# Sixteen meta tokens as full-height products over zeroed rows, in retention and in latent attention

## The chip, the cores and the metric

The kernel runs on one core of a Trainium2 chip. A core has a matrix engine (TensorE, written PE in the profile, with its weight loads listed apart as PEld), a vector engine (DVE), a scalar engine (ACT), a general engine (POOL) and a queue for transfers (SP). Each engine works through its own list of instructions in order and waits for others by semaphores. The metric is the time of one execution of the program on the device, in microseconds (us); lower is better.

## The reference

Two blocks run one after the other on 256 tokens of width 1024. The first has two layers, each with a feed-forward network, a mixer (gated delta rule in one layer, sliding-window attention in the other) and a second feed-forward network. The second block puts 16 learned "meta" tokens ahead of the 256 and has one layer: a mixer made of bidirectional retention (8 heads) and latent attention (8 heads) side by side, and a feed-forward network. Only the 256 real tokens are returned. The change touches the mixer of the second block alone:

```python
def _retention_dir(q, k, v, log_gamma, inclusive):      # o_i = sum_j gamma^(i-j) (q_i . k_j) v_j
    ...
    scores = jnp.einsum('bnihd,bnjhd->bnhij', qc, kc) * dmask
    inner = jnp.einsum('bnhij,bnjhe->bnihe', scores, vc)
    ...
def _mla_attention(q_nope, q_rope, k_nope, k_rope, v):
    ...
        s = jnp.einsum('bqhd,bkhd->bhqk', qn, k_nope) + jnp.einsum('bqhr,bkr->bhqk', qr, k_rope)
        p = jax.nn.softmax(s.astype(jnp.float32) * scale, axis=-1).astype(v.dtype)
        return jnp.einsum('bhqk,bkhd->bqhd', p, v)
def _mixer(...):
    ...
    y_ret = _head_group_norm(_bidir_retention(rq, rk, rv, decay_f, decay_b), gn_w)
    y_ret = (jax.nn.silu(rg) * y_ret) @ w_ret_out
    ...
    y_mla = _mla_attention(...).reshape(B, L, MLA_HEADS * MLA_DV) @ w_mla_out
    merged = jax.nn.sigmoid(a_gret) * y_ret + jax.nn.sigmoid(a_gmla) * y_mla
    return merged @ w_o
```

So every query looks at 272 keys: 256 real ones and 16 meta ones. In both mixers the last step of a head is a sum over those 272 keys, weights times values.

## The kernel before, in words

All activations live in on-chip memory, transposed (model dimension on the 128 partitions). Weights are streamed from memory in pieces of 512 columns. Each piece is split by ACT (`whi`, line 355) and DVE (`wlo`, line 356) into a high and a low part, and each linear layer (`lin`, lines 373 to 375) makes three products per 128 rows of weights: high by high, low by high, high by low. These triples are most of what TensorE does.

The mixer of the second block, `retention_mla`, has two parts. **Retention** goes over four pairs of heads. For a pair, `rope` turns keys and queries, `val` transposes the values of each head into a tile `rv` with three slices (128 keys, 128 keys, 16 meta keys), and `ret` makes the decayed scores, again with three slices, in a tile `ptr` of DVE's writing. The 16 meta rows of the second head of a pair sit 32 partitions further down than those of the first. `weigh` (line 1130) then sums over the keys: for each of two heads and two blocks of 128 queries, three products into one accumulating bank, over 128, 128 and 16 rows. An fp32 product is issued as two matmul records, so one `weigh` is 12 products and 24 records, and there are four of them. Group norm (`bn_stats` on DVE, a power on POOL) and `close` follow.

**Latent attention** goes over eight heads in an order written out by hand, `MLA_PLAN`: `s` scores and softmax of a head, `t` its transposition (the weights become `pt`, two slices of 128 keys copied by ACT at line 1339 and 16 meta rows copied by DVE at line 1340), `w` the weighing of one head (line 1350), and `y` one block of the retention output's linear layer. The plan names heads, so `w0` to `w7`. The weighing of a head is three products over 128, 128 and 16 rows, 64 columns of output and 256 queries, six records; the even head of a pair writes partitions 0 to 63 of a bank, the odd head 64 to 127. After the odd head, `split` makes `oh` and `ol` out of the bank. The scheduler of the language may move an instruction past others of its engine where it expects a wait.

The sliding-window attention of the first block has a weighing of the same kind (line 979): two heads into the two halves of a bank, each by products over 128 rows with 64 columns of output, there with 512 columns moved.

POOL has little to do. In this part it adds up squares for the norms (line 407), takes powers (line 383) and zeroes tiles (`MEMSET`).

Of the kernel before, what the change touches and what calls it, by code (L numbers as in the profile page):

```python
# [10 lines left out]
F32R = mybir.dt.float32r  # L11
I32 = mybir.dt.int32
AF = mybir.ActivationFunctionType
ALU = mybir.AluOpType
# [3 lines left out]
P = 128  # L18
D = 1024
KD = 8  # L20
S = 256
# [29 lines left out]
    "y0 s1 s0 y1 s6 t0 s2 t1 w0 w1 t2 s3 y2 s4 y3 t3 w2 w3 t4 s5 y4 w4 s7 t5 y5 t6 y6 t7 w5 w6 y7 w7"  # L51
# [170 lines left out]
def kernel(ctx: ExitStack, tc: tile.TileContext, dram: dict, out: bass.AP, dump=None):  # L222
# [79 lines left out]
    def tab(name, rows=P):  # L302
        o, w = _TABS[name]
        return tabs[:rows, o : o + w]
# [724 lines left out]
    def retention_mla(norm, stats, finish, dec, after):  # L1029
        xs = norm.xs  # L1030
        Y = [None] * H
        with home("mx") as gp:
            with home("ret") as rp:
# [20 lines left out]
                A.copy(rotr, tab("rot"))  # L1054
                metak = [[sb(rp, [P, 48], f"metak{j}{i}", F32R) for i in range(2)] for j in range(2)]
# [26 lines left out]
                def val(t, hh):  # L1082
# [6 lines left out]
                    o = sb(rp, [P, 3, P], f"rv{hh}", bufs=2)  # L1089
                    A.copy(o[:, 0:2, :], b[:, 0:2, :])  # L1090
                    A.copy(o[m - NM : m, 2, :], b[m - NM : m, 2, :])
                    return o
# [6 lines left out]
                def ret(p, k, q):  # L1099
# [3 lines left out]
                    for hh in range(2):  # L1103
# [7 lines left out]
                        pt = sb(rp, [P, 3, S], f"ptr{hh}", bufs=2)  # L1111
                        d3 = dec.t[2 * p + hh]
                        V.scalar_tensor_tensor(pt[:, 0:2, :], b, 64 ** -0.5, d3[:, 0:2, :], op0=ALU.mult, op1=ALU.mult)
                        pts.append(pt)
# [4 lines left out]
                    for hh in range(2):  # L1119
                        m = slice(32 * hh, 32 * hh + NM)  # L1120
                        V.scalar_tensor_tensor(pts[hh][m, 2, :], b[m, :], 64 ** -0.5, dec.t[2 * p + hh][m, 2, :], op0=ALU.mult, op1=ALU.mult)
# [34 lines left out]
                for p in range(4):  # L1156
# [13 lines left out]
                    vals[p] = val(v0, 0), val(v1, 1)  # L1170
# [29 lines left out]
            with home("mla") as rp:  # L1200
# [109 lines left out]
                PT, OB = {}, {}  # L1310
# [19 lines left out]
                def turn(h):  # L1330
# [7 lines left out]
                    pt = sb(rp, [P, 3, S], "pt", bufs=3)  # L1338
                    A.copy(pt[:, 0:2, :], b)
                    V.tensor_copy(pt[:NM, 2, :], bm)  # L1340
                    PT[h] = pt

                def weigh(h):
                    pr, hf = h // 2, h % 2
                    if hf == 0:
                        OB[pr] = bank(pm, [P, S])
                    o = OB[pr][hf * 64 : hf * 64 + 64, :]
                    for c in range(3):
                        m = P if c < 2 else NM
                        mm(o, VN[:m, c, h * 64 : h * 64 + 64], PT[h][:m, c, :], start=c == 0, stop=c == 2)  # L1350
                    if hf:
                        oh = sb(rp, [P, S], f"oh{pr}", F32R)
                        ol = sb(rp, [P, S], f"ol{pr}", F32R)
                        split(OB[pr], oh, ol)
                        MO.append((oh, ol))
# [184 lines left out]
```

## Time and profile before

| | |
|---|---|
| time before, median of 3 runs | 1481.27 us (1472.56 to 1790.16) |
| the profiled execution, its own time | 1473.83 us |
| its span, first to last instruction | 1472.0 us |
| granted TensorE clock, mean over the span | 0.995 |
| PE busy / DVE busy / ACT busy / POOL busy | 1443.5 / 1107.7 / 858.2 / 114.1 us |
| retention | about 1031 to 1127 us of the span |
| latent attention up to the end of the plan | about 1127 to 1204 us |
| gates, output and the last feed-forward network | about 1204 to 1472 us |

A busy time counts an instruction from its start to its end, and products overlap: a product of 0.28 us starts 0.11 us after the one before it. So a busy TensorE says little by itself. What a product costs is read from the distance of its start to the start of the next one, and below this distance is called its pitch.

### The profile page before, as it was taken

How to read it: one execution, taken by the hardware profiler on the slowest of the kernel's cores; microseconds unless marked ns; L12 is line 12 of the kernel's file. 1: busy time of each engine (PE TensorE's matmuls, PEld its weight loads, DVE VectorE, ACT ScalarE, POOL GpSimd, SP SyncE). 2: the span in 40 equal slices, each digit the busy share in tenths (PEclk: the TensorE clock that was granted, in tenths of full speed). 3: DMA queues.
4: the chain of work that ended last, by engine and by line, in shares of the span. 5: the costliest groups of instructions: out<-in, count | busy, mean ns of one | idle time of the engine just before them, and what ended most of it. 6: DMA issues, size and time to landing. Idle time of an engine off the chain costs nothing.

```text
span 1472.0 us, 31018 instructions
## 1 busy us (share of the span) xinstructions
PE 1443.5 (98%) x12318; PEld 1405.1 (95%) x12318; DVE 1107.7 (75%) x2340; ACT 858.2 (58%) x1767; POOL 114.1 (8%) x123
## 2 busy tenths in 40 slices
PE   8999999998999999999999999999999999999997
PEld 8999999988999999999997999999999889999997
DVE  6877668886877767777678877788877758777764
ACT  6655567655655555555547655665545756665552
POOL 2000141101100010000100100012001000100000
PEclk9999999999999999999999999999999999999998
DMA  7655443551555555555550555555432425555551
GB/s 254 224 195 201 171 148 116 166 167 33 181 191 198 201 189 185 201 195 187 193 199 30 201 178 195 177 196 172 134 113 91 144 87 195 207 199 187 193 197 58
DMA packets 46368, 248.34 MB, mean 169 GB/s; under 512 B 11408, under 2 KB 16272, under 8 KB 17168
## 3 DMA queue, kind: packets, MB, share of 16 engines
q1 hardware_dynamic: 45680, 245.87, 49.0%
q8 instruction: 97, 1.59, 0.4%
q10 hardware_dynamic: 544, 0.50, 0.1%
q14 instruction: 47, 0.39, 0.1%
HBM read 243.99 MB, written 2.36 MB: 167 GB/s over the span
## 4 chain that ended last, share of the span: by engine, by line
PE 86%; DVE 7%; ACT 2%; DMA 2%; issue 1%; POOL 1%; DVEq 0%; POOLq 0%; ACTq 0%; SPq 0%
PE bank L375 26%; PE bank L373 26%; PE bank L374 26%; DVE wlo L356 2%; PE bank L1130 1%; PE bank L1350 1%; DVE cv L652 1%; ACT whi L355 1%; PE bank L979 1%; DMA tc<-s 1%; PE bank L1319 1%; DVE xl L395 0%; DMA s<-tb 0%; PE bank L969 0%; POOL rr L383 0%
## 5 line engine op out<-in xcount | busy, mean ns | idle before, releaser
L356 DVE TENSOR_TENSOR wlo<-raw,whi 128x512 fp32r<-128x512 f32 x922 | 641.2, 700 | 257.4 <-ACT whi L355 255.9
L355 ACT CAST whi<-raw 128x512 fp32r<-128x512 f32 x922 | 565.4, 618 | 444.8 <-PE bank L375 407.3
L373 PE MATMUL bank<-xh,whi 128*128 128x256 f32 (+1 forms) x2488 | 697.0, 280 | 1.3 <-DVE xt L513 1.0
L374 PE MATMUL bank<-xh,wlo 128*128 128x256 f32 (+1 forms) x2488 | 692.9, 279 | 2.1 <-DVE wlo L356 2.1
L375 PE MATMUL bank<-xl,whi 128*128 128x256 f32 (+1 forms) x2488 | 692.3, 278 | 1.1 <-DVE xl L395 1.0
L374 PEld LDWEIGHTS bank<-xh,wlo 128*128 128x128 f32 x2488 | 468.5, 188 | 3.6 <-DVE wlo L356 3.1
L373 PEld LDWEIGHTS bank<-xh,whi 128*128 128x128 f32 x2488 | 466.9, 188 | 4.2 <-issue 2.1
L375 PEld LDWEIGHTS bank<-xl,whi 128*128 128x128 f32 x2488 | 466.9, 188 | 2.2 <-DVE xl L395 1.7
L375 PE MATMUL bank<-al,whi 128*128 128x256 f32 x880 | 243.8, 277 | 0.0
L373 PE MATMUL bank<-ah,whi 128*128 128x256 f32 x880 | 243.8, 277 | 0.0
L374 PE MATMUL bank<-ah,wlo 128*128 128x256 f32 x880 | 243.8, 277 | 0.0
L374 PEld LDWEIGHTS bank<-ah,wlo 128*128 128x128 f32 x880 | 165.9, 189 | 0.0
L375 PEld LDWEIGHTS bank<-al,whi 128*128 128x128 f32 x880 | 165.2, 188 | 0.0
L373 PEld LDWEIGHTS bank<-ah,whi 128*128 128x128 f32 x880 | 165.2, 188 | 0.0
L407 POOL TENSOR_TENSOR ssq<-sq,ssq 128x256 f32<-128x256 f32 (+1 forms) x72 | 63.8, 886 | 1080.4 <-ACT sq L406 1070.8
L378 ACT CAST ah<-ffu 128x256 fp32r<-128x256 f32 x110 | 44.7, 407 | 26.2 <-DVE ffu L482 26.1
L482 DVE TENSOR_TENSOR ffu<-ffg,ffu 128x256 f32<-128x256 f32 x110 | 46.7, 425 | 4.6 <-ACT ffg L481 1.2
L478 DVE TENSOR_TENSOR ffg<-bank,r 128x256 f32<-128x256 f32 x110 | 46.6, 424 | 2.8 <-PE bank L375 2.2
L481 ACT ACTIVATE ffg<-ffg 128x256 f32<-128x256 f32 x110 | 45.3, 414 | 5.7 <-DVE ffg L478 5.4
L480 DVE TENSOR_TENSOR ffu<-bank,r 128x256 f32<-128x256 f32 x110 | 46.6, 423 | 0.3
L379 DVE TENSOR_TENSOR al<-ffu,ah 128x256 fp32r<-128x256 f32 x110 | 46.0, 418 | 0.5 <-ACT ah L378 0.5
L373 PE MATMUL bank<-dec,whi 128*128 128x256 f32 x128 | 36.7, 286 | 0.0
(360 smaller groups left out, 1426.4 us busy)
## 6 DMA issues: line engine op xcount, KB each, us to landing
raw<-gu SPq DMA_DIRECT2D x109, 1024.0 KB, 4.8
raw<-dn SPq DMA_DIRECT2D x55, 1024.0 KB, 4.9
raw<-wret SPq DMA_DIRECT2D x12, 1024.0 KB, 4.9
raw<-aqk SPq DMA_DIRECT2D x8, 1024.0 KB, 4.8
raw<-wga SPq DMA_DIRECT2D x8, 1024.0 KB, 4.8
raw<-bin SPq DMA_DIRECT2D x6, 1024.0 KB, 4.9
raw<-az SPq DMA_DIRECT2D x4, 1024.0 KB, 4.8
raw<-av SPq DMA_DIRECT2D x4, 1024.0 KB, 4.9
```

The source lines that it names most:

```text
L355: A.copy(hi[:, :n], raw[:, o : o + n])
L356: V.tensor_tensor(lo[:, :n], raw[:, o : o + n], f32(hi[:, :n]), op=ALU.subtract)
L373: mm(o, wh, xh[:, :n], start=k == 0, stop=False)
L374: mm(o, wl, xh[:, :n], start=False, stop=False)
L375: mm(o, wh, xl[:, :n], start=False, stop=k == last)
L378: A.copy(hi, src)
L379: V.tensor_tensor(lo, src, f32(hi), op=ALU.subtract)
L407: G.tensor_tensor(acc[:, :n], q[:, :n], acc[:, :n], op=ALU.add)
L478: V.tensor_tensor(g, pg, r[:, :S], op=ALU.mult)
L480: V.tensor_tensor(u, pu, r[:, :S], op=ALU.mult)
L481: A.activation(g, g, AF.Silu)
L482: V.tensor_tensor(u, g, u, op=ALU.mult)
```

## The change

Both weighings get 128 rows in place of 16. The 16 meta rows move out of the third slices of `ptr`, `rv` and `pt` into tiles of their own, `metap` (weights) and `metav` (values), whose other rows are zeroed once by POOL: eight tiles for retention (two sets of two heads) and four for latent attention, where the third slice of the values `VN` is zeroed as well. In latent attention `w` now names a pair, and goes over the key slices outside and the two heads inside.

```diff
-    "y0 s1 s0 y1 s6 t0 s2 t1 w0 w1 t2 s3 y2 s4 y3 t3 w2 w3 t4 s5 y4 w4 s7 t5 y5 t6 y6 t7 w5 w6 y7 w7"
+    "y0 s1 s0 y1 s6 t0 s2 t1 w0 t2 s3 y2 s4 y3 t3 w1 t4 s5 y4 s7 t5 y5 w2 t6 y6 t7 y7 w3"
...
+                metap = [[sb(rp, [P, S], f"metap{j}{hh}") for hh in range(2)] for j in range(2)]
+                metav = [[sb(rp, [P, P], f"metav{j}{hh}") for hh in range(2)] for j in range(2)]
+                for t in metap[0] + metav[0] + metap[1] + metav[1]:
+                    G.memset(t, 0.0)
...
-                    A.copy(o[:, 0:2, :], b[:, 0:2, :])
-                    A.copy(o[m - NM : m, 2, :], b[m - NM : m, 2, :])
+                    A.copy(o, b[:, 0:2, :])
+                    mv = metav[p % 2][hh]
+                    A.copy(mv[m - NM : m, :], b[m - NM : m, 2, :])
...
-                            for c in range(3):
-                                m = slice(0, P) if c < 2 else slice(32 * hh, 32 * hh + NM)
-                                mm(bs[hh][:, i, :], pts[hh][m, c, i * P : i * P + P], rv[hh][m, c, :], start=c == 0, stop=c == 2)
+                            q = slice(i * P, i * P + P)
+                            for c in range(2):
+                                mm(bs[hh][:, i, :], pts[hh][0][:, c, q], rv[hh][0][:, c, :], start=c == 0, stop=False)
+                            mm(bs[hh][:, i, :], pts[hh][1][:, q], rv[hh][1], start=False, stop=True)
...
                 VN = sb(rp, [P, 3, 512], "vnat")
+                G.memset(VN[:, 2, :], 0.0)
+                metap = [sb(rp, [P, S], f"metap{j}") for j in range(4)]
+                for t in metap:
+                    G.memset(t, 0.0)
...
-                    A.copy(pt[:, 0:2, :], b)
-                    V.tensor_copy(pt[:NM, 2, :], bm)
-                    PT[h] = pt
+                    A.copy(pt, b)
+                    V.tensor_copy(metap[h % 4][:NM, :], bm)
+                    PT[h] = pt[:, 0, :], pt[:, 1, :], metap[h % 4]
...
-                def weigh(h):
+                def weigh(pr):
...
                     for c in range(3):
-                        m = P if c < 2 else NM
-                        mm(o, VN[:m, c, h * 64 : h * 64 + 64], PT[h][:m, c, :], start=c == 0, stop=c == 2)
-                    if hf:
...
+                        for hf in range(2):
+                            h = 2 * pr + hf
+                            mm(b[hf * 64 : hf * 64 + 64, :], VN[:, c, h * 64 : h * 64 + 64], PT[h][c], start=c == 0, stop=c == 2)
```

What this makes of the lists of the engines, at three places. On TensorE, at the weighing of the first pair of heads in retention, before (the products of `lin` around it are of the next pair's projections):

```order
L375 MATMUL bank_14498<-xl_2692_14140,whi_14517 128x272
L1130 MATMUL bank_14535<-rv_2752_14428,ptr_2762_14481 128x128 x6
L1130 MATMUL bank_14536<-rv_2754_14435,ptr_2764_14490 128x128 x6
L373 MATMUL bank_14567<-xh_2564_13369,whi_14568 128x256
```

The same place after:

```order
L375 MATMUL bank_14514<-xl_2692_14140,whi_14533 128x272
L1136 MATMUL bank_14551<-rv_2760_14444,ptr_2770_14497 128x128 x2
L1137 MATMUL bank_14551<-metav_2721_14294,metap_2717_14290 128x128
L1136 MATMUL bank_14551<-rv_2760_14444,ptr_2770_14497 128x128 x2
L1137 MATMUL bank_14551<-metav_2721_14294,metap_2717_14290 128x128
L1136 MATMUL bank_14552<-rv_2762_14451,ptr_2772_14506 128x128 x2
L1137 MATMUL bank_14552<-metav_2722_14295,metap_2718_14291 128x128
L1136 MATMUL bank_14552<-rv_2762_14451,ptr_2772_14506 128x128 x2
L1137 MATMUL bank_14552<-metav_2722_14295,metap_2718_14291 128x128
L373 MATMUL bank_14583<-xh_2564_13369,whi_14584 128x256
```

Nothing moves; the third product of each group reads other tiles. The other engines' lists in retention keep their order too, but for POOL's (below).

On TensorE, at the weighing of the first pair of heads in latent attention (`tabs,pe` are transpositions of the softmax weights, `dec,whi` products of the retention output's linear layer), after:

```order
L1349 MATMUL bank_16278<-tabs_81,pe_16172 128x128 x4
L1349 MATMUL bank_16279<-tabs_81,pe_16172 16x128 x2
L1361 MATMUL bank_16289<-pt_16260,vnat_15926 64x256
L375 MATMUL bank_16326<-dec_2877_15019,whi_16329 128x256
L1361 MATMUL bank_16289<-pt_16286,vnat_15926 64x256
L1361 MATMUL bank_16289<-pt_16260,vnat_15926 64x256
L1361 MATMUL bank_16289<-pt_16286,vnat_15926 64x256
L1361 MATMUL bank_16289<-metap_3074_15928,vnat_15926 64x256
L1361 MATMUL bank_16289<-metap_3075_15929,vnat_15926 64x256
L373 MATMUL bank_16326<-dec_2945_15350,whi_16345 128x256
```

Before, the six products stood together, three of one head and then three of the other, and the product of `lin` came behind them. Now one product of `lin` stands behind the first of the six, and the five behind it alternate between the heads. In the second pair three transpositions stand at that place; in the third and fourth pair the six stand together, behind a block of the linear layer.

On POOL, at the end of the feed-forward network ahead of retention, after (`ssq` are the sums of squares of the norm, `rms` its power):

```order
L407 TENSOR_TENSOR ssq_13378<-sq_14041,ssq_13378 128x272
L1059 MEMSET metap_2717_14290 128x256
L1059 MEMSET metap_2718_14291 128x256
L1059 MEMSET metav_2721_14294 128x128
L1059 MEMSET metav_2722_14295 128x128
L1059 MEMSET metap_2719_14292 128x256
L1059 MEMSET metap_2720_14293 128x256
L1059 MEMSET metav_2723_14296 128x128
L1059 MEMSET metav_2724_14297 128x128
L407 TENSOR_TENSOR ssq_13375<-sq_14145,ssq_13375 128x256
L407 TENSOR_TENSOR ssq_13378<-sq_14149,ssq_13378 128x272
L383 TENSOR_TENSOR rms_14154<-rms_14154,mhalf_85 128x8
```

The eight new `MEMSET` stand ahead of the last two sums of squares; before, nothing stood between the rows above and below them. The five new ones of latent attention (128x512 and four of 128x256) stand behind the `MEMSET` of 128x384 and ahead of two of 128x512 that were there before.

## Rows read from the trace of the kernel before

**Rows 1.** The page: busy time, share of the span and instructions of each engine.

```profile
PE 1443.5 (98%) x12318; PEld 1405.1 (95%) x12318; DVE 1107.7 (75%) x2340; ACT 858.2 (58%) x1767; POOL 114.1 (8%) x123
```

**Rows 2.** Stretches: length, then busy (count) of PE, PEld, DVE, ACT, POOL; clock; transfers.

```profile
580.00:730.00 150.00, 150.00 (x1326) 150.00 (x1325) 109.69 (x200) 86.52 (x160) 3.51 (x4) 1.00 0.57 194
850.00:1000.00 150.00, 150.00 (x1276) 150.00 (x1275) 117.42 (x224) 90.53 (x174) 8.50 (x8) 1.00 0.55 187
1035.00:1130.00 95.00, 95.00 (x753) 89.11 (x752) 75.79 (x198) 43.87 (x99) 5.57 (x8) 1.00 0.33 109
1204.00:1284.00 80.00, 80.00 (x707) 80.00 (x708) 64.91 (x123) 51.09 (x100) 5.19 (x7) 1.00 0.55 189
1284.00:1460.00 176.00, 176.00 (x1555) 176.00 (x1554) 123.59 (x227) 95.79 (x175) 6.34 (x7) 1.00 0.51 172
```

**Rows 3.** Timeline of PE, retention: first start, length to last end, line, form, count.

```profile
1042.34 4.18 PE L1130 MATMUL bank<-rv,ptr 128*128 128x128 f32 x24
1046.45 0.38 PE L373 MATMUL bank<-xh,whi 128*128 128x256 f32 x1
...
1042.56 0.39 PE L1130 MATMUL bank<-rv,ptr 128*128 128x128 f32 x2
1042.67 0.58 PE L1130 MATMUL bank<-rv,ptr 128*128 128x128 f32 x2
1042.88 0.37 PE L1130 MATMUL bank<-rv,ptr 16*128 16x128 f32 x1
1043.93 0.48 PE L1130 MATMUL bank<-rv,ptr 16*128 16x128 f32 x2
```

**Rows 4.** Timeline of PE, latent attention, the first pair and a single head.

```profile
1167.52 3.23 PE L1350 MATMUL bank<-pt,vnat 128*64 128x256 f32 x12
1170.67 0.39 PE L375 MATMUL bank<-dec,whi 128*128 128x256 f32 x1
...
1167.78 0.38 PE L1350 MATMUL bank<-pt,vnat 128*64 128x256 f32 x1
1168.00 0.38 PE L1350 MATMUL bank<-pt,vnat 128*64 128x256 f32 x1
1168.21 0.38 PE L1350 MATMUL bank<-pt,vnat 128*64 128x256 f32 x1
1168.52 0.42 PE L1350 MATMUL bank<-pt,vnat 16*64 16x256 f32 x1
...
1185.99 1.65 PE L1350 MATMUL bank<-pt,vnat 128*64 128x256 f32 x6
1187.57 0.95 PE L1319 MATMUL bank<-kf,qf 128*128 128x272 f32 x3
```

**Rows 5.** Timeline of PE, sliding-window attention, its weighing of one and of two heads.

```profile
803.45 1.07 PE L979 MATMUL bank<-pt,vn 128*64 128x512 f32 x2
804.45 0.33 PE L969 MATMUL bank<-tabs,pe 128*128 128x128 f32 x1
...
810.24 2.62 PE L979 MATMUL bank<-pt,vn 128*64 128x512 f32 x8
812.79 0.39 PE L373 MATMUL bank<-oh,whi 128*128 128x256 f32 x1
```

**Rows 6.** Timeline of ACT and DVE: the weights of the pair's second head are copied.

```profile
1167.40 0.59 ACT L1339 COPY pt<-bank 128x512 f32<-128x512 f32 x1 [0.69 <-PE bank L1337]
1167.91 0.40 DVE L1340 COPY pt<-bank 16x256 f32<-16x256 f32 x1
```

**Rows 7.** Timeline of PE and POOL: the end of the feed-forward network, and zeroing.

```profile
1015.10 0.28 PE L375 MATMUL bank<-al,whi 128*128 128x256 f32 x1
1017.03 1.54 POOL L407 TENSOR_TENSOR ssq<-sq,ssq 128x256 f32<-128x256 f32 x1 [3.16 <-ACT sq L406]
1021.13 0.74 PE L413 MATMUL bank<-ones,ssq 128*128 128x1 f32 x6 [0.70 <-POOL ssq L407]
1125.06 1.01 POOL L1278 MEMSET pt<- 128x512 f32 x2
```

More of the change, by code (lines that the diff above doesn't have):

```diff
@@ L1080, in rope, with val @@
                     return oh, ol
-                def val(t, hh):
+                def val(p, t, hh):
                     b = bank(pm, [P, 3, P])
@@ L1088, in val @@
                     nc.tensor.transpose(b[:m, 2, :], t[:, ST - m : ST], ident)
-                    o = sb(rp, [P, 3, P], f"rv{hh}", bufs=2)
-                    A.copy(o[:, 0:2, :], b[:, 0:2, :])
-                    A.copy(o[m - NM : m, 2, :], b[m - NM : m, 2, :])
-                    return o
+                    o = sb(rp, [P, 2, P], f"rv{hh}", bufs=2)
+                    A.copy(o, b[:, 0:2, :])
+                    mv = metav[p % 2][hh]
+                    A.copy(mv[m - NM : m, :], b[m - NM : m, 2, :])
+                    return o, mv
                 def gate(i, hh):
@@ L1110, in ret @@
                             mm(b[:, c, :], kl[rows, cs], qh[rows, :], start=False, stop=True)
-                        pt = sb(rp, [P, 3, S], f"ptr{hh}", bufs=2)
+                        pt = sb(rp, [P, 2, S], f"ptr{hh}", bufs=2)
                         d3 = dec.t[2 * p + hh]
-                        V.scalar_tensor_tensor(pt[:, 0:2, :], b, 64 ** -0.5, d3[:, 0:2, :], op0=ALU.mult, op1=ALU.mult)
-                        pts.append(pt)
+                        V.scalar_tensor_tensor(pt, b, 64 ** -0.5, d3[:, 0:2, :], op0=ALU.mult, op1=ALU.mult)
+                        pts.append((pt, metap[p % 2][hh]))
                     b = bank(pm, [48, S])
@@ L1120, in ret @@
                         m = slice(32 * hh, 32 * hh + NM)
-                        V.scalar_tensor_tensor(pts[hh][m, 2, :], b[m, :], 64 ** -0.5, dec.t[2 * p + hh][m, 2, :], op0=ALU.mult, op1=ALU.mult)
+                        V.scalar_tensor_tensor(pts[hh][1][m, :], b[m, :], 64 ** -0.5, dec.t[2 * p + hh][m, 2, :], op0=ALU.mult, op1=ALU.mult)
                     return pts
@@ L1169, in retention_mla @@
                     g0 = gate(6 * p + 4, 0)
-                    vals[p] = val(v0, 0), val(v1, 1)
+                    vals[p] = val(p, v0, 0), val(p, v1, 1)
                     g1 = gate(6 * p + 5, 1)
@@ L1309, in retention_mla @@
                 MO = []
-                PT, OB = {}, {}
+                PT = {}
                 def scores(h):
@@ L1337, in turn @@
                             nc.tensor.transpose(o, pe[:, i, c * P : c * P + m], ident)
-                    pt = sb(rp, [P, 3, S], "pt", bufs=3)
-                    A.copy(pt[:, 0:2, :], b)
-                    V.tensor_copy(pt[:NM, 2, :], bm)
-                    PT[h] = pt
-                def weigh(h):
[L1344 to L1347, printed above, removed]
-                    for c in range(3):
-                        m = P if c < 2 else NM
-                        mm(o, VN[:m, c, h * 64 : h * 64 + 64], PT[h][:m, c, :], start=c == 0, stop=c == 2)
-                    if hf:
[L1352 to L1355, printed above, removed]
+                    pt = sb(rp, [P, 2, S], "pt", bufs=3)
+                    A.copy(pt, b)
+                    V.tensor_copy(metap[h % 4][:NM, :], bm)
+                    PT[h] = pt[:, 0, :], pt[:, 1, :], metap[h % 4]
+                def weigh(pr):
+                    b = bank(pm, [P, S])
+                    for c in range(3):
+                        for hf in range(2):
+                            h = 2 * pr + hf
+                            mm(b[hf * 64 : hf * 64 + 64, :], VN[:, c, h * 64 : h * 64 + 64], PT[h][c], start=c == 0, stop=c == 2)
+                    oh = sb(rp, [P, S], f"oh{pr}", F32R)
+                    ol = sb(rp, [P, S], f"ol{pr}", F32R)
+                    split(b, oh, ol)
+                    MO.append((oh, ol))
                 YR = []
```

## The prediction

> **What bounds the kernel now.** I read the page first: TensorE has work for 98% of the span, the next engine, DVE, for 75% [rows 1]. A busy share does not say that TensorE is the bound, so the second view is the busy time by stretch, over the part that the change touches and what follows it [rows 2]. There TensorE has something in flight in every microsecond, at full clock, DVE is at four fifths and transfers at a third to a half. The reader is to see that work taken off TensorE's list here shortens the kernel, as long as its operands come in time. The third view is the timeline of TensorE at the two weighings, since what a product costs is its pitch, the distance to the next start.
>
> In retention, products over 128 rows start 0.11 us apart (1042.56, 1042.67), but the first one over 16 rows comes 0.21 after the last over 128, and from there to the first 16-row record of the next group are 1.05 us [rows 3]. A group is six records; at 0.11 each it would take 0.67. So 0.38 of each group goes to the changes from 128 to 16 rows and back. That it is the form and not a late operand is seen in the count: all four groups of a weighing have it, though only the first can wait for data. A whole weighing takes 4.11 us from its first start to that of the next product (1042.34 to 1046.45).
>
> In latent attention a record over 128 rows, 64 columns out and 256 columns moved has a pitch of 0.215 us (1167.78, 1168.00, 1168.21), and the step to the 16-row record is 0.31. A head of six records takes 1.58 us (1185.99 to 1187.57) and a pair 3.15 (1167.52 to 1170.67) [rows 4]: the two heads stand strictly behind each other. There are eight heads in five stretches, so 12.6 us in all.
>
> **The change part by part.**
>
> *Retention.* 32 of the 96 records get 128 rows. With nothing left to change form, a weighing is 24 records at 0.111, 2.66 us, in place of 4.11: 1.45 less. The first product of `lin` behind it is 0.38 long [rows 3], where another is 0.28 [rows 7]; I put that to the last change of form: 0.1. That is 1.55 us for each of four weighings, 6.2 us. Below nothing this term cannot go unless full rows cost more than 0.11, and the rows with full rows show 0.11; its bounds are 5.8 and 6.3.
>
> *Latent attention, rows.* Without the step to 16 rows and back a head would be six records at 0.215 and one exit: about 1.4 us.
>
> *Latent attention, two heads at once.* The two heads of a pair write different halves of the output partitions, so they use different columns of the array. Whether two such products run side by side is not seen at line 1350, where a 16-row record always stands between the heads. It is seen at line 979: one head's two records take 1.00 us (803.45 to 804.45), and two heads' eight records take 2.55 (810.24 to 812.79) [rows 5]. In line, eight records at twice the 0.215 of 256 columns, with an exit, would be 3.5 or more. So they do overlap there, and the second head's records must have run between the first head's. I take that for line 1350, whose shape differs only in moving 256 columns. A pair whose six products stand together is then one head's chain, 0.27 + 4 x 0.215 = 1.13, plus a start of the second head 0.1 to 0.25 later, plus an exit like the step above, 0.31: 1.6 us. That holds for the third and fourth pair, which stand behind a block of the linear layer.
>
> The first two pairs follow the transposition of their second head at once. Its weights are copied from 1167.40 to 1167.99 by ACT and 1167.91 to 1168.31 by DVE [rows 6], while the pair starts at 1167.52. Before, the first head's 1.58 us covered this. Now the second product needs that copy about 0.5 us after the first began. The scheduler put one product of `lin` (first pair) or three transpositions (second pair) there. That fills the wait, but it changes the form twice. I count, for the first pair, 0.57 to the foreign product, 0.2 through it, then the second head's chain of 1.13 and the exit 0.31, less the 0.11 that the foreign product costs anyway: 2.1 us; for the second pair likewise 2.15. Queued behind the waiting product on TensorE is only the pair's own rest and then `lin`, whose pieces lie ready. Sum after: 2.1 + 2.15 + 1.6 + 1.6 = 7.45 against 12.6, so 5.2 us less. The bounds: without any overlap a pair is 12 x 0.215 and 0.15 for entry and exit, 2.73, and the two split ones some 0.25 more, 11.4 in all, which leaves 1.2; with full overlap everywhere 6.4, which gives 6.2.
>
> *Zeroing.* Two 512-column `MEMSET` take 1.01 us on POOL [rows 7], so I estimate 0.25 for 256 columns and 0.14 for 128: 1.6 us for the eight of retention. They can begin when the feed-forward network's last product (1015.10, 0.28 long) has left the memory, and end near 1017.0; the sum of squares now queued behind them began at 1017.03. If POOL runs at half that speed, they end at 1018.6 and that sum 1.6 us later than before. TensorE took the sums at 1021.13 after a wait of 0.70, so part of it is covered; I count 0.2, with 0 and 1.6 as bounds. The five of latent attention (1.5 us) delay two `MEMSET` by as much, whose tiles are needed only after two more blocks of `lin`, about 5 us. Nothing; without that cover 1.5.
>
> *Nothing else.* DVE and ACT keep their instructions; copies go to another tile. A plan with four weighings opens 4 stretches in place of 5, which is within the above.
>
> The sum: 6.2 + 5.2 - 0.2 = 11.2 us off the profiled execution of 1473.83: 1462.6, so 1463. That execution lies 7.4 below the median shown (1481.27) and 1.3 above the fastest run; I set the forecast against it. Here 2% is 29 us, about what a measurement of this kernel can tell from no change, so the gain, 0.8%, is far inside.
>
> **A rule against a row.** The row says that two heads of 128 rows each overlapped at line 979 [rows 5]. The Trainium skill, page "TensorE: Matmul & The Clock Gate", Part 3, "The mechanism", says that a weight load overlaps running products only where the row group differs, and that products start in strict order; both heads here use all row groups, so by it the interleaving gains nothing. The measured 2.55 us speaks against it, hence its small chance below. The same skill's page "TensorEngine Tiling (Array Packing)", Key Properties, says that a change of tiling mode, not of tile, drains the engine, which the 0.21 at each change of rows agrees with.
>
> **The rivals.**
>
> *The heads do not overlap at 256 columns.* For it: no row has this shape side by side. Against it: line 979. Latent attention then saves 1.2, and if every product starts as late as the first of a stretch does, 0.26 to 0.27 (1167.52 to 1167.78 [rows 4]), 12 x 0.27 a pair makes it lose 0.8. Sum 5.2 to 7.2 off, 1466.6 to 1468.6: say 1467.
>
> *A long stretch falls into a slow pace.* From 580 to 730 TensorE starts 1326 products of the same shape, from 850 to 1000 only 1276, both at clock 1.00 and with no wait [rows 2]: 113.1 against 117.6 ns. The pace changes after a stall or a change of form and then stays for a whole network. The trace does not show what sets it. The 2262 products from 1204 to 1460 run at the fast pace now [rows 2]. What the change moves ahead of them could tip them: 2262 x 4.4 ns = 10 us. If the fast parts of the 753 in retention go too, 2 to 3 us more, and the kernel ends at 1473 to 1475, not faster or slower than before. It decides from 11.2 / 0.0044 = 2,550 products on. For a smaller part, one of the two stretches, the time is 1466 to 1470. Between runs it may differ as well: 7.4 us between the profiled execution and the median run is about the 6.9 that 1555 products make.
>
> *The network before falls into the fast pace.* 1276 products in 150 us from about 835 to 1031 make 7.3 us: 1455. Nothing in the change touches it.
>
> *Zeroing holds up the norm.* The sums, the power and the row factors of the whole opening wait behind POOL. At half speed with the wait exhausted it costs 1.5 to 3: 1465. For an end above 1474 POOL would have to be 11 us late, seven times the 1.6 estimated.
>
> **How the numbers follow.** Forecast as summed 0.50; no overlap 0.10; slow pace in part 0.15, in whole 0.05; fast pace ahead 0.12; zeroing 0.05; something not seen 0.03. The range from 1455 to 1473 leaves out about 0.1 above and some of the fast pace below; the forecast's own range, from the bounds of its terms, is 1461 to 1467. Beyond 2% either way only what I have not seen can lead: faster 0.02, same 0.96, slower 0.02.
>
> **What would show each step.** In the profile after: a weighing in retention from its first start to that of the next product at 2.7 us, no 16-row form among its records; in latent attention 1.6 us for a pair that stands together and 2.1 to 2.2 for the first two; starts of the two heads nearer than 0.2; POOL's eight `MEMSET` over before 1018 and TensorE's wait for the sums below 1; products per stretch in 1204 to 1460 as now. Wrong it would be if the weighings shrink and the end does not move (then something else is late next, or the pace has changed), or if a pair still takes 2.7.

## The result and the profile after

The changed kernel takes 1456.5 us (median of four executions, 1455.2 to 1458.1), against 1482.9 for the kernel before beside it: a ratio of 0.985, with a 95% interval from 0.981 to 0.989. Two executions of the kernel before, one of 1790 us here and one of 2403 us at a mean clock of 0.55 among its repetitions, lie far above all others, and the ratios leave them out (the 1482.9 does not). Timed again later, with twelve executions against 35 of the kernel before, the ratio is 0.992 (0.989 to 0.995); the plain medians, 1468.1 and 1474.8, stand half of that apart. So it is faster by about one per cent, less than the 2% below which the prediction spoke of no difference. The profiled execution takes 1458.1 by the clock and has a span of 1456.3, 15.7 less than the 1472.0 of before. Where these 15.7 us went is the question of this section; only some ten of them turn out to belong to the change.

First the page's line of busy time of the changed kernel, in the order of [rows 1], and then its busy time by stretch, with the columns of [rows 2]. The stretches are laid where the same work stands.

```profile
PE 1426.7 (98%) x12318; PEld 1396.2 (96%) x12318; DVE 1106.2 (76%) x2340; ACT 858.5 (59%) x1767; POOL 116.3 (8%) x136
```

```profile
580.00:730.00 150.00, 150.00 (x1326) 150.00 (x1325) 109.69 (x201) 86.98 (x161) 3.49 (x4) 1.00 0.58 196
850.00:1000.00 150.00, 150.00 (x1326) 150.00 (x1325) 121.36 (x231) 94.68 (x183) 8.75 (x10) 1.00 0.57 196
1030.00:1120.00 90.00, 90.00 (x761) 87.78 (x761) 76.36 (x202) 44.41 (x99) 6.99 (x13) 1.00 0.34 115
1188.00:1268.00 80.00, 80.00 (x708) 79.47 (x705) 64.70 (x123) 51.16 (x100) 5.02 (x7) 1.00 0.54 185
1268.00:1445.00 177.00, 177.00 (x1564) 177.00 (x1563) 124.35 (x228) 95.82 (x175) 6.50 (x8) 1.00 0.51 173
```

TensorE still has work for 98% of the span, with the same 12318 products, and POOL has thirteen instructions more, the zeroings. The second row of the stretches is the one to look at: from 850 to 1000, in a network that the change does not touch, TensorE now starts 1326 products where it started 1276 [rows 2]. The pace there is the fast one, and that alone shortens this network from 202.8 to 196.1 us; the window attention ahead of it takes 68.2 in both.

The weighing of retention, in the timeline of TensorE after the change (start, length to the last end, line, form, count):

```profile
1038.52 0.60 PE L1136 MATMUL bank<-rv,ptr 128*128 128x128 f32 x4
1038.96 0.39 PE L1137 MATMUL bank<-metav,metap 128*128 128x128 f32 x2
1039.18 0.61 PE L1136 MATMUL bank<-rv,ptr 128*128 128x128 f32 x4
...
1040.97 0.39 PE L1137 MATMUL bank<-metav,metap 128*128 128x128 f32 x2
1041.11 0.37 PE L373 MATMUL bank<-xh,whi 128*128 128x256 f32 x1
1041.32 0.28 PE L374 MATMUL bank<-xh,wlo 128*128 128x256 f32 x1
```

A group of six records takes 0.66 us (1038.52 to 1039.18) where it took 1.05 [rows 3], no 16-row form is left, and the whole weighing takes 2.59 us to the start of the next product, against 4.11. The first linear product behind it is still a long one, 0.37 against 0.38, and 0.21 passes to its neighbour.

Latent attention, same view: the first pair, with one foreign product put between its first and its other products, and the third, which stands together.

```profile
1157.94 0.65 PE L1361 MATMUL bank<-pt,vnat 128*64 128x256 f32 x2
1158.51 0.38 PE L375 MATMUL bank<-dec,whi 128*128 128x256 f32 x1
1158.83 0.86 PE L1361 MATMUL bank<-pt,vnat 128*64 128x256 f32 x5
...
1160.27 0.38 PE L373 MATMUL bank<-dec,whi 128*128 128x256 f32 x1
...
1178.86 1.08 PE L1361 MATMUL bank<-pt,vnat 128*64 128x256 f32 x8
1179.78 0.60 PE L1361 MATMUL bank<-metap,vnat 128*64 128x256 f32 x4
1180.31 0.88 PE L1349 MATMUL bank<-tabs,pe 128*128 128x128 f32 x6
```

Twelve records in 1.45 us (1178.86 to 1180.31), where six records took 1.58 [rows 4]: the two heads run side by side. The first pair, split by a foreign product, takes 2.33 (1157.94 to 1160.27).

The opening of retention lost time. TensorE's rows there, and then busy time and clock (the number behind POOL's, 0.50) of the stretch in which it lost it, and the same of the kernel before at that place of its opening:

```profile
1015.75 0.74 PE L413 MATMUL bank<-ones,ssq 128*128 128x1 f32 x6 [0.82 <-POOL ssq L407]
...
1017.62 0.43 PE L373 MATMUL bank<-xh,whi 128*128 128x272 f32 x1
1017.84 0.43 PE L374 MATMUL bank<-xh,wlo 128*128 128x272 f32 x1
...
1020.56 0.43 PE L374 MATMUL bank<-xh,wlo 128*128 128x272 f32 x1
...
1022.47 0.28 PE L374 MATMUL bank<-xh,wlo 128*128 128x272 f32 x1
...
1023.71 0.28 PE L375 MATMUL bank<-xl,whi 128*128 128x272 f32 x1
```

```profile
1017.60:1021.00 3.40, 3.40 (x17) 3.40 (x16) 1.29 (x2) 1.42 (x3) 1.28 (x1) 0.50 0.22 34
```

```profile
1023.00:1026.50 3.50, 3.50 (x29) 3.35 (x28) 2.44 (x5) 1.58 (x3) 1.24 (x1) 1.00 0.30 47
```

After the sums of squares the granted clock falls to 0.50, the 1.2 GHz level, for 15 linear products. Their pitch is 0.227 us (twelve from 1017.84 to 1020.56) where it is 0.124 at full clock (ten from 1022.47 to 1023.71). That is 15 x 0.103 = 1.55 us, in a stretch in which the kernel before kept 1.00.

All of it in one table. Each mark is the start of a named record in the trace: the last product of the third and of the fourth of the five feed-forward networks (line 375; the kernel names the fourth 21, and the texts below call it the 21st), the first and the last record of retention's weighings, the first and the last of latent attention's, and the end of the span.

| us | before | after | difference |
|---|---|---|---|
| start to the end of the third network | 744.10 | 745.32 | +1.2 |
| window attention and fourth network | 271.00 | 264.29 | -6.7 |
| opening of retention, to its first weighing | 27.24 | 28.91 | +1.7 |
| retention, first to last weighing | 78.08 | 72.15 | -5.9 |
| to the first weighing of latent attention | 47.09 | 47.27 | +0.2 |
| latent attention, first to last weighing | 36.00 | 30.63 | -5.4 |
| to the end | 268.53 | 267.75 | -0.8 |
| from the end of the fourth network to the end | 456.95 | 446.71 | -10.2 |

The change can act only behind the fourth network. There the profile gains 10.2 us, against 11.2 forecast; the other 5.5 of the 15.7 lie ahead of it, 6.7 of pace in the fourth network less 1.2 lost before. And not all of the 10.2 is TensorE's: from the last weighing to the last linear product (line 375) both kernels take 257.0 us, so the 0.8 of the last stretch comes behind that product, where the final norm and the output stand (11.6 us before, 10.8 after). Up to it the gain is 9.5.

### The profile page after: what moved, and what is told of

Read it like the earlier page. It is cut to its first block, busy times and chain, and to the rows that moved or that the text cites. A ratio compares the mean times of both kernels' runs of the same rounds, so it can differ in the third digit from the quotient of the medians.

```text
span 1456.3 us, 31032 instructions
## 1 busy us (share of the span) xinstructions
PE 1426.7 (98%) x12318; PEld 1396.2 (96%) x12318; DVE 1106.2 (76%) x2340; ACT 858.5 (59%) x1767; POOL 116.3 (8%) x136
## 4 chain that ended last, share of the span: by engine, by line
PE 87%; DVE 7%; ACT 3%; DMA 1%; issue 1%; POOL 1%; SPq 0%; DVEq 0%; POOLq 0%; ACTq 0%
PE bank L373 26%; PE bank L375 26%; PE bank L374 26%; DVE wlo L356 2%; ACT whi L355 1%; DVE cv L652 1%; PE bank L979 1%; PE bank L830 1%; PE bank L1331 1%; PE bank L1136 0%; PE bank L1361 0%; DVE xl L395 0%; PE bank L969 0%; POOL rr L383 0%; DMA xt<-xt 0%
```

## The experiments

Times of whole executions spread by about 1% with nothing changed, so the experiments are read by the stretches of the table.

**The two kernels again.** The kernel before, unchanged:

> The kernel before once more, unchanged, to see what differs between two executions of one program. Theory A (the pace of a long stretch of linear products is set anew at each execution by the stall ahead of it): the 21st feed-forward network, 117.8 ns a product in the profile of before, may run at 113.3 here; then its stretch is about 7 us shorter and the times spread by up to some 10 us with nothing changed. Theory B (the pace belongs to the program): 117.8 ns again there, 113.3 in the other long stretches, span within 1 us of 1472.

Its profiled execution is the one of 2403 us, so its stretches can't be set beside the others, and it does not tell theory A from B. Nine more executions took 1468.5 to 1483.3 us: 15 us of spread with nothing changed, twice what one network's pace makes. The changed kernel, unchanged:

> The changed kernel once more, unchanged. Theory A: the network ahead of retention may run at 117.8 ns this time, and the end then comes about 7 us later than 1456; retention from first to last weighing 72.2 us and latent attention 30.6 us whatever that pace is. Theory B: 113.3 ns there again. On the opening of retention, where 15 linear products ran at a granted clock of 0.50 and took 1.55 us more than at full clock: if the eight zeroings ahead of the last sums of squares bring this (they moved the sums by 0.1 us), it comes again; if it is chance, it is gone and the opening takes 27.3 us from the network's last product to the first weighing, not 28.9.

The pace differs between executions of one program, as theory A has it; that a stall ahead sets it is not shown. The network ahead of retention ran at the slow pace this time, 271.07 us with the window attention, by the same program that had run it in 264.29:

```profile
850.00:1000.00 150.00, 150.00 (x1276) 150.00 (x1275) 116.77 (x222) 90.15 (x174) 6.24 (x6) 1.00 0.52 187
```

1276 products, as in the kernel before [rows 2], at the same clock of 1.00. Yet retention took 72.15 and latent attention 30.63 again, to the hundredth, and from the network's end to the end of the span 446.88 us passed (446.71). The span was 1469.8, 13.4 longer than in the first profile of the same program. The half clock in the opening came again: 28.94 us.

**Each part alone.** Retention's part, with latent attention as before:

> Retention's part of the change alone (full rows over zeroed tiles there; latent attention as before). If the parts add: first to last weighing in retention 72.2 us (78.1 before), latent attention 36.0 as before, and from the network's last product to the end 5.8 to 6.2 us less than before, plus 1.6 if the opening falls to half clock again as theory 'the zeroings bring it' has it. If the gain of the whole came from elsewhere: less than 3 us.

```diff
-                 m = slice(0, P) if c < 2 else slice(32 * hh, 32 * hh + NM)
-                 mm(bs[hh][:, i, :], pts[hh][m, c, i * P : i * P + P], rv[hh][m, c, :], ...)
+             mm(bs[hh][:, i, :], pts[hh][1][:, q], rv[hh][1], start=False, stop=True)
...
```

Retention 72.15, latent attention 36.00, opening 28.95. Behind the network 453.38 us, which is 3.6 less than before: 5.9 gained in the weighings, 1.7 lost in the opening, 0.6 in the stretches between and behind. By time nothing is to be seen: 0.9996 (0.997 to 1.003), an interval that 3.6 us (0.0024) lie within. Latent attention's part alone:

> Latent attention's part alone (full rows, both heads in one step, new plan; retention as before, no zeroing there). If the parts add: first to last weighing of latent attention 30.6 us (36.0 before), retention 78.1 as before, from the network's last product to the end 5.2 to 5.4 us less than before. With no zeroing ahead of the sums the opening of retention stays at 27.2 us and full clock, if it is the zeroings that bring the half clock; if it is chance, it may fall here too.

Latent attention 30.63, retention 78.08, opening 27.25 at full clock, behind the network 451.76: 5.2 less than before, and 0.996 (0.993 to 0.9995) by time. The parts come to 3.6 + 5.2 = 8.8 against 10.2 of the whole. The difference stands behind the last linear product, where 11.8 and 11.9 us pass with either part and 10.8 in the whole; why the end differs stays open. Up to that product the parts save 3.8 and 5.5 and the whole 9.5, so there they add.

**What makes latent attention faster.** The changed kernel does three things there at once: full rows, one step for both heads, and products of the two heads by turns. With full rows and one step, but the second head queued behind the first:

> Latent attention's part alone, with full rows and one step for the pair, but the second head's three products queued behind the first head's three instead of alternating with them. Theory X (two chains in different column halves run side by side wherever they stand near each other in the queue): a pair that stands together takes 1.4 to 1.6 us as in the changed kernel, first to last weighing 30.6 us or less. Theory Y (products start strictly in the order of the queue, so that only the neighbours of two heads overlap): 0.26 + 10 x 0.209 + 0.31 = 2.7 us a pair, 34 to 35.5 us from first to last. Theory Z (in between: part of the second chain overlaps): about 2 us a pair.

```diff
-     for c in range(3):
-         for hf in range(2):
+     for hf in range(2):
+         for c in range(3):
```

```profile
1195.10 1.13 PE L1353 MATMUL bank<-pt,vnat 128*64 128x256 f32 x6
1196.01 0.38 PE L1353 MATMUL bank<-metap,vnat 128*64 128x256 f32 x1
1196.07 0.38 PE L1353 MATMUL bank<-pt,vnat 128*64 128x256 f32 x1
...
1196.50 0.59 PE L1353 MATMUL bank<-metap,vnat 128*64 128x256 f32 x2
1197.03 0.55 PE L1341 MATMUL bank<-tabs,pe 128*128 128x128 f32 x3
```

In the timeline of TensorE the pair takes 1.93 us (1195.10 to 1197.03), 0.48 more than with turns: the second head's chain still runs beside the first, but starts about half a microsecond behind it. The first pair takes 1.97 and the second 2.32. From first to last weighing it is 31.48 us. Theory Z, the one in between, comes nearest; for a strict queue, 2.7 a pair, it is too short by far.

With turns and one step, but the third product over 16 rows:

> Latent attention's part alone, both heads alternating in one step, but the third product of each head over its 16 rows as before. If the change of rows costs latent attention what it cost it before: 0.26 + 3 x 0.209 + 0.31 into the 16 rows, 0.215, and an exit of 0.3 to 0.4: 1.7 to 1.8 us a pair that stands together instead of 1.44, first to last weighing 31.6 to 32.2 us instead of 30.6. If nothing is lost: 1.44 and 30.6. If the two heads no longer overlap at all once rows change: 3.1 a pair, 36.

```diff
- mm(b[...], VN[:, c, ...], PT[h][c], ...)
+ mm(b[...], VN[: P if c < 2 else NM, c, ...], PT[h][c][: P if c < 2 else NM], ...)
```

```profile
1198.67 1.08 PE L1353 MATMUL bank<-pt,vnat 128*64 128x256 f32 x8
1199.69 0.65 PE L1353 MATMUL bank<-metap,vnat 16*64 16x256 f32 x4
1200.27 0.55 PE L1341 MATMUL bank<-tabs,pe 128*128 128x128 f32 x3
```

A pair takes 1.60 (1198.67 to 1200.27), and first to last 31.05: the change of rows costs 0.15 a pair, since both heads now pay it at the same time. I expected 1.7 to 1.8. With full rows alone, head by head under the plan of before:

> Latent attention with full rows over zeroed tiles, but weighed head by head under the plan of before. There heads 0 and 1, 2 and 3, and 5 and 6 stand next to each other in the queue (always different halves of the columns), heads 4 and 7 alone. If neighbours overlap in part, as when the second head was queued behind the first in one step (1.93 to 2.3 us a pair): first to last weighing 36.0 - 2 x 1.0 - 1.2 - 2 x 0.2 = 32.4 us, so most of the gain comes from the full rows alone. If neighbours overlap only when queued alternately: six chains of full rows with one exit less, 36.0 - 8 x 0.2 - 3 x 0.15, about 34 us.

```diff
- m = P if c < 2 else NM
- mm(o, VN[:m, c, h * 64 : h * 64 + 64], PT[h][:m, c, :], ...)
+ mm(o, VN[:, c, h * 64 : h * 64 + 64], PT[h][c], ...)
```

```profile
1186.45 1.08 PE L1353 MATMUL bank<-pt,vnat 128*64 128x256 f32 x4
1187.37 0.59 PE L1353 MATMUL bank<-metap,vnat 128*64 128x256 f32 x2
1187.89 0.50 PE L1323 MATMUL bank<-kf,qf 128*128 128x272 f32 x1
```

```profile
1196.45 1.14 PE L1353 MATMUL bank<-pt,vnat 128*64 128x256 f32 x6
1197.37 0.38 PE L1353 MATMUL bank<-metap,vnat 128*64 128x256 f32 x1
1197.42 0.38 PE L1353 MATMUL bank<-pt,vnat 128*64 128x256 f32 x1
...
1198.38 0.38 PE L373 MATMUL bank<-dec,whi 128*128 128x256 f32 x1
```

32.50 us from first to last, 3.5 of the 5.4 gained, where 32.4 was expected. A single head takes 1.44 (1186.45 to 1187.89; 1.58 before), which is what a pair takes when its heads go by turns. Two neighbours take 1.93 (1196.45 to 1198.38; 3.16 before; the first two pairs 1.97 and 2.32), though the plan names no pairs: the 16-row record between them had kept them apart. So the edits overlap in what they bring. Full rows alone give 3.5; one step for the pair, heads in line, 1.0 more; turns 0.9 more. Turns without full rows give 4.95 of the 5.37.

**What the zeroings cost.** The kernel before with retention's eight tiles zeroed at the changed kernel's place, and used by nothing:

> The kernel before, with retention's eight tiles allocated and zeroed on POOL at the place where the changed kernel does it, and used by nothing. Theory 'the zeroings bring the half clock': TensorE waits 0.82 us for the last sums of squares instead of 0.70, some 15 linear products of the opening run at a pitch of 0.227 us, and from the network's last product to the first weighing 28.9 us pass instead of 27.2; retention 78.1 and latent attention 36.0 as before. Rival 'it belongs to the full rows or to a shifted time': full clock, 27.2 to 27.4 us.

> The kernel before with the eight zeroings and nothing else, once more. There DVE's scaling took 1.54 us, TensorE waited 1.61 us for the sums and yet kept its full clock. If the memory places of this program set that: 1.54 and 1.61 again, 28.2 us from the network's last product to the first weighing, full clock. If it is chance of one execution: 0.75, 0.82, half clock and 28.9 us.

```diff
+ metap = [[sb(rp, [P, S], f"metap{j}{hh}") for hh in range(2)] for j in range(2)]
+ metav = [[sb(rp, [P, P], f"metav{j}{hh}") for hh in range(2)] for j in range(2)]
+ for t in metap[0] + metav[0] + metap[1] + metav[1]:
+     G.memset(t, 0.0)
```

One program, two outcomes. In the first execution the opening took 28.24 us, with a wait of 1.61 for the sums and full clock; in the second 29.01, with a wait of 0.82 and half clock. So the zeroings alone, with no full row, bring a loss, 1.0 us by the wait or 1.8 by wait and clock, which answers the rival of the first text; the fixed memory places that the second text offers are answered too. How the wait comes is in DVE's timeline: the scaling of the last decay block, in the kernel before, the changed kernel, and the first run of the zeroings alone.

```profile
1015.82 0.61 DVE L1024 TENSOR_SCALAR dec<-tabs,nlg 128x768 f32<-128x768 f32 x1
```

```profile
1010.33 0.75 DVE L1024 TENSOR_SCALAR dec<-tabs,nlg 128x768 f32<-128x768 f32 x1
...
1014.00 0.34 DVE L1473 TENSOR_SCALAR xt<-xt,colv 128x256 f32<-128x256 f32 x1
```

```profile
1014.30 1.54 DVE L1024 TENSOR_SCALAR dec<-tabs,nlg 128x768 f32<-128x768 f32 x1
```

POOL's timeline, first its last sum in the kernel before, then the zeroings and the last two sums in the changed kernel:

```profile
1020.32 0.76 POOL L407 TENSOR_TENSOR ssq<-sq,ssq 128x272 f32<-128x272 f32 x1 [1.75 <-ACT sq L406]
```

```profile
1009.95 0.57 POOL L1059 MEMSET metap<- 128x256 f32 x2 [1.25 <-DVE wlo L356]
1010.45 0.76 POOL L1059 MEMSET metav<- 128x128 f32 x2
1011.16 0.56 POOL L1059 MEMSET metap<- 128x256 f32 x2
1011.67 0.35 POOL L1059 MEMSET metav<- 128x128 f32 x2
1011.99 1.20 POOL L407 TENSOR_TENSOR ssq<-sq,ssq 128x256 f32<-128x256 f32 x1
1014.94 0.76 POOL L407 TENSOR_TENSOR ssq<-sq,ssq 128x272 f32<-128x272 f32 x1 [1.75 <-ACT sq L406]
```

Beside POOL's zeroings DVE's scaling takes 0.75 or 1.54 us where it takes 0.61 in every other place. POOL is slower beside it as well: the two `MEMSET` of 128x128 that run beside the scaling take 0.76, the two later ones 0.35. DVE's queue behind the scaling is late, by 0.12 at the scaled `xt` (1014.00, which is 4.39 after the network's last product; 4.27 before), whose square ACT makes and POOL adds to the last sum. TensorE's wait grows from 0.70 [rows 7] to 0.82. The Trainium skill, page "Advanced Engine Details and Errata", section "VectorE Performance Modes", says that the vector engine's second port is shared with POOL, and that POOL's instructions and those vector instructions that use both ports block each other. That POOL and DVE hold each other up is what these rows show too, with 0.14 to 0.93 us as the price on DVE; that this scaling uses both ports no row shows.

The zeroing put behind the norm:

> The changed kernel with retention's eight tiles zeroed behind the norm (a product with 0 of the row factors on POOL) instead of ahead of the last sums of squares. If the 0.12 us that the zeroings add to TensorE's wait are what tips the clock: wait 0.70, full clock, 27.2 us from the network's last product to the first weighing, and from that product to the end 445.1 us (446.7 and 446.9 with the zeroings ahead). If the clock falls for another cause: 28.9 us again. If the late zeroing holds up the values: the first weighing comes 1 us or more later than 27.2. By time, 1.6 us are 0.1% and may drown in the differences of pace.

```diff
- for t in metap[0] + metav[0] + metap[1] + metav[1]:
-     G.memset(t, 0.0)
+ for t, n in [(t, n) for j in range(2) for ts, n in ((metap[j], S), (metav[j], P)) for t in ts]:
+     G.tensor_scalar(t, r[:, :n], 0.0, None, op0=ALU.mult)
```

```profile
1026.17 0.74 PE L413 MATMUL bank<-ones,ssq 128*128 128x1 f32 x6 [0.69 <-POOL ssq L407]
```

```profile
1028.00:1031.50 3.50, 3.50 (x29) 3.35 (x28) 2.41 (x5) 1.62 (x3) 1.30 (x2) 1.00 0.23 54
```

In TensorE's timeline the wait is 0.69, and in the stretch behind it the clock is 1.00. The opening takes 27.30 us, and 445.52 pass behind the network, 1.2 to 1.4 less than in the changed kernel (1.6 to 1.8 up to the last linear product). DVE's scaling took 0.61 again, with the same tiles allocated, so it is the writing beside it that counts. By time, 0.992 (0.989 to 0.995), not to be told from it, as expected. Half of the zeroings put there:

> The changed kernel with the first pair's four tiles zeroed ahead of the last sums of squares and the second pair's behind the norm. DVE's scaling of the last decay block took 0.75 us beside eight zeroings and 0.61 with none. If POOL's writing beside DVE is what delays the sums: 0.61 to 0.75 there, TensorE's wait 0.70 to 0.82. If the clock falls whenever tiles are zeroed there: some 15 products at half clock and 28.9 us from the network's last product to the first weighing. If it takes the full delay of 0.12: full clock, 27.3 us.

DVE's scaling took 0.90, the wait was 0.96, and the clock fell: 29.14 us, so four tiles cost no less than eight. I had expected a wait between 0.70 and 0.82; how much two engines hinder each other depends on more than how much is written.

**Both edits that help.** The zeroing behind the norm, and the first two pairs weighed one transposition later:

> The changed kernel with two edits: retention's tiles zeroed behind the norm, as in the run before, and a plan in which the first two pairs are weighed after one more transposition, so that their six products stand together. If a pair that stands together takes 1.44 us everywhere and what was put between its products costs 0.1 to 0.2 elsewhere: first to last weighing of latent attention (starting later, since the first pair moves back) no longer a measure; from the end of retention's last weighing to that of latent attention 77.2 us, against 77.9 in the changed kernel; from the network's last product to the end 444.8 to 445.1, against 446.7 and 446.9. If the later weighing or the copies hold up what follows: 445.5 or more. By time 0.99 of before, like the changed kernel, within the spread of pace.

```diff
- ... s6 t0 s2 t1 w0 t2 s3 y2 s4 y3 t3 w1 t4 s5 ...
+ ... s6 t0 s2 t1 t2 w0 s3 y2 s4 y3 t3 t4 w1 s5 ...
```

```profile
1158.42 1.08 PE L1361 MATMUL bank<-pt,vnat 128*64 128x256 f32 x8
1159.33 0.60 PE L1361 MATMUL bank<-metap,vnat 128*64 128x256 f32 x4
1159.87 0.72 PE L1331 MATMUL bank<-kf,qf 128*128 128x272 f32 x2
```

All four pairs take 1.45 us (1158.42 to 1159.87 the first). From retention's last weighing to latent attention's last, 77.0 us pass, against 77.9, and 444.2 behind the network: 2.5 less than in the changed kernel, 12.7 less than before (11.9 up to the last linear product). By time it is 0.991 (0.988 to 0.995), which does not tell it from the changed kernel.

The stretches of all these profiles, one kernel a row; the last column is the part of the one before it that comes behind the last linear product:

| us | window and fourth network | opening | wait for sums | behind the network | its end |
|---|---|---|---|---|---|
| before | 271.00 | 27.24 | 0.70 | 456.95 | 11.56 |
| changed | 264.29 | 28.91 | 0.82 | 446.71 | 10.78 |
| changed, again | 271.07 | 28.94 | 0.83 | 446.88 | 10.81 |
| retention alone | 271.07 | 28.95 | 0.83 | 453.38 | 11.79 |
| latent attention alone | 271.08 | 27.25 | 0.70 | 451.76 | 11.87 |
| zeroing alone | 264.28 | 28.24 | 1.61 | 457.30 | 11.07 |
| zeroing alone, again | 270.99 | 29.01 | 0.82 | 458.00 | 11.04 |
| zeroing later | 271.01 | 27.30 | 0.69 | 445.52 | 11.20 |
| four ahead | 264.27 | 29.14 | 0.96 | 446.93 | 10.79 |
| heads in line | 264.27 | 27.34 | 0.70 | 453.14 | 12.32 |
| 16 rows | 264.27 | 27.34 | 0.70 | 452.36 | 11.82 |
| full rows only | 270.99 | 27.34 | 0.69 | 453.57 | 11.60 |
| both edits | 264.33 | 27.31 | 0.69 | 444.23 | 10.79 |

## Why the prediction was right, and where it was not

**The number.** 1463 was forecast and 1456.5 came, inside the range of 1455 to 1473 and at the edge of it, because two of the cases came together: the forecast and the rival "the network before falls into the fast pace". So far it is luck: the next profiled execution of the same program took 1471.6. That rival was put at 1455 and 7.3 us; the network got 6.7 shorter. The repetition shows that it has nothing to do with the change: the same program ran it slowly the next time, and the 13 profiles have it fast six times and slow seven, in kernels with the change and without. Its chance of 0.12 was too low for six in 13; the two counts in [rows 2] had shown both paces in one execution, and that should have been read as "either, next time". The repeated timing, free of that luck by its number of executions, gives 0.992 of the profiled 1473.83, or 1462 (1467 by the plain medians).

**Retention: right.** 6.2 us forecast, 5.9 measured. A weighing is 1.52 shorter (4.11 to 2.59), where 1.45 was worked out; four of them make 6.1, of which the table's row holds 5.9, since it ends at the start of the last record (0.17 more is saved there). The stretch behind is 0.2 longer even so; its cause stays open. The 0.1 added for the linear product behind it did not come: 0.37 against 0.38. So it is not the step from 16 rows that makes that product long.

**Latent attention: sum right, terms off.** 5.2 forecast, 5.4 measured. Pairs that stand together take 1.45, not 1.6, since the second head starts with the first (within 0.01 us) rather than 0.1 to 0.25 behind it. The split ones take 2.33 and 2.50 with the foreign products in them; the prediction's 2.1 and 2.15 leave out what those cost anyway, 0.11 for the linear product and, by an estimate from transpositions in a row, which start 0.11 apart, 0.33 for the three. Less that, the split pairs took 2.2 each; the first is 0.1 over its forecast, since the way through the foreign product took 0.32 (1158.51 to 1158.83) and not 0.2. Together 7.45 was forecast and 7.3 came. The rival "no overlap", drawn from the rule of the Trainium skill's page "TensorE: Matmul & The Clock Gate", Part 3, falls with the twelve records in 1.45 us: both heads used all rows, in different columns, and ran side by side. The rule speaks of weight loads; that turns gain nothing was the prediction's inference from it. That the overlap was read from line 979 [rows 5] rather than left to the rule was the step that held. What it did not see is the credit: full rows alone give 3.5 of the 5.4, and with turns they are worth only 0.4.

**Zeroing: wrong, 0.2 for 1.7.** The step put the loss into POOL's queue: a sum of squares that waits behind the zeroings, partly covered by a wait of TensorE. The queue did no harm: the eight took 2.1 us (1009.95 to 1012.02; 1.6 estimated) and the first sum behind them began 0.45 later, but the last sum comes when its square is ready, after 1.75 of waiting for ACT in both kernels. What failed is the step "Nothing else", by which DVE keeps its instructions and the sum has no term for their times: one of them got 0.14 longer beside POOL, and the 0.12 that reached TensorE was followed by half clock, 1.55 us. The 1.7 lies just above this term's upper bound of 1.6, which had been worked out for another mechanism. The named sign, a wait below 1, was fulfilled at 0.82 and said nothing: the clock of the stretch behind the wait had to be looked at.

**The other stretches: right within 1 us.** The one behind latent attention is 0.8 shorter, all of it behind the last linear product, and the one between 0.2 longer. With retention's part alone this one is 0.4 longer (47.51) and with latent attention's alone 0.1 shorter (46.95), so the five zeroings of latent attention cost nothing there, as forecast. The rival of a slow pace in the long stretch behind the change, with a chance of 0.20, never came: that stretch took 267.8 to 269.3 us in all 13 profiles.

## What to carry to other kernels

A product over a few rows between products over all of them cost more here than the rows it saved, and head by head it also kept neighbours in other columns from running side by side; price it by the pitch on both of its sides. Where executions of one program differ by more than the change is worth, compare stretches between the same records, and repeat the kernel before and the changed one before crediting the change with a stretch that it does not touch. An instruction on an idle engine was not free here: look at what its neighbour on DVE takes beside it, and at the granted clock behind the wait that it lengthens.

## What the runs showed of the hardware that was not expected

The clock after a short wait: in the five profiles in which TensorE waited 0.82 to 0.96 us for the last sums of squares, 12 to 16 linear products behind it ran at the 1.2 GHz level; in the seven with 0.69 or 0.70 all ran at full clock. The one with 1.61 kept its full clock too, so the length of the wait is not the whole of it; what else decides was not settled. Falls to 0.50 come elsewhere too (near 212 and 335 us in the changed kernel), and at places that differ between executions of one program (218 and 280 us with the zeroing alone; 19, 275 and 333 in its second execution), so the link to the zeroings rests on the count: five of the six profiles that have them there, none of the seven that don't.

Two paces at the same clock: the 256-column products of a long stretch start 113.1 or 117.6 ns apart (1326 or 1276 in 150 us), both at 1.00, and keep to it for a whole network. Which one it is changes from one execution to the next in the fourth network; the first and the second ran slowly in four of the 13 profiles each, the third and the last in none. Its cause stays open.

Two chains in different halves of the columns run side by side without being queued by turns, about half a microsecond apart (1.93 us a pair); by turns they start together, and the second head is then free: 1.45 for two, 1.44 for one.
